# Forgetting heads: the mask moves from a matrix product to a GpSimd select, and the low parts of the probabilities move from VectorE to GpSimd

## The chip, the cores and the metric

The kernel runs on one core of one Trainium2 chip. The metric is the device time of one execution in microseconds (us). Three runs before the change took 1156.0, 1157.74 and 1158.17 us; their median is 1157.74. Engines are named as the profile names them: PE (TensorE, products), PEld (its weight loads), DVE (VectorE), ACT (ScalarE), POOL (GpSimd), SP (the queue that issues most DMAs).

## The reference

One decoder layer on 2048 tokens of width 1024: a normalised and modulated input goes through one input projection; eight forgetting-attention heads (FoX) and eight sliding-window heads run on it; their gated outputs go through one output projection and are added to the input. The change touches the forgetting heads only:

```python
cum = jnp.cumsum(jax.nn.log_sigmoid(f_logit), axis=1)      # per head
...
s = einsum('bhqd,bhkd->bhqk', qb, kh) * scale
s = s + cb[..., None] - cum[:, :, None, :]
causal = key_pos[None, :] <= q_pos[:, None]
s = jnp.where(causal, s, -jnp.inf)
p = jax.nn.softmax(s, axis=-1)
return einsum('bhqk,bhkd->bhqd', p, vh)
```

## The kernel before

The layer is computed in float32 accuracy with float16 operands: most values are split into a high part in float16 and a low part (the rest, also in float16), and a product is done as three (high by high, high by low, low by high). The program has a start (loads, norms), a stage of sliding-window heads, a stage of forgetting heads (some 462 to 1003 us) and the output projection.

The order of every engine's instructions is written out by hand. In the forgetting stage a loop (L1671) goes over 160 steps: 8 heads, in each 4 chunks of 512 queries, in each the pairs of 128-key blocks up to the diagonal (20 steps a head). A step's tile has keys on partitions and queries along the row. Its parts are methods of `Step`:

- `scores` (L1341): for each of the two key blocks two products into the score tile `sta` in PSUM, T with T (L1349) and the forget-gate rows (L1350). Where a block lies on the diagonal, a third product (L1352) of an identity `identb` and a constant `dmaskT`, both bfloat16, adds -1e30 to the masked scores of the 128x128 diagonal square. There is one score tile of two banks, so the next step's scores wait for this step's exponential.
- `exp32` (L1354): ACT turns the scores into float32 probabilities `p32` (called p in the profile; L1356). Three such tiles go round.
- `high` (L1358): ACT copies p to float16, the high part `pha` (L1360). Three tiles go round.
- `low` (L1362): DVE subtracts the high part from p and writes the low part beside it (L1363).
- `pv` (L1365): for each 128x128 block three products with the values (L1373, L1375 with the high part, L1376 with the low part).

Of the two blocks of a step either none lies on the diagonal (row width 1024) or both do; then the rows are cut to what the mask leaves, 512 + 384 = 896 or 256 + 128 = 384. Each chunk ends in one step of each of these two kinds, so 64 of the 160 steps are diagonal.

Step s runs in this order: exponential of s; low part of s-1; half of the filling work; high part of s; scores of s+1; products with values of s-2; the other half of the filling work. The filling work is projections of later heads (L351), row maxima (PE L1300, DVE L1303 and L1305), gates (ACT tanh L396, DVE L392, DMA of `z_d` from POOL L394), splits of weights (L273; ACT L1442 and DVE L1443 for the output weights) and, in head 7, the first output products (L1576). POOL's queue in this stage holds only DMA issues: weights (`wr`, L221), the maximum of a weight tile out to DRAM (`mx_d`, L230) and back to all partitions (`mxr`, L235), which waits for the first to land, pieces of a gate weight (`gw`, L1231), and `z_d`. In the sliding-window stage POOL also runs selects (L932, L934).

Of the kernel before, what the change touches and what calls it, by code (L numbers as in the profile page):

```python
# [10 lines left out]
F32 = mybir.dt.float32  # L11
F16 = mybir.dt.float16
BF16 = mybir.dt.bfloat16
I16 = mybir.dt.int16
I32 = mybir.dt.int32
AF = mybir.ActivationFunctionType
ALU = mybir.AluOpType
AX = mybir.AxisListType

P = 128  # L20
# [9 lines left out]
NEG = -1.0e30  # L30
# [5 lines left out]
XM, XR, VW = 66, 69, 129  # L36
# [7 lines left out]
def hybrid_layer(  # L44
# [17 lines left out]
    V, A, G, PE, SP = nc.vector, nc.scalar, nc.gpsimd, nc.tensor, nc.sync  # L62
# [12 lines left out]
    const = ctx.enter_context(tc.tile_pool(name="const", bufs=1))  # L75
# [78 lines left out]
    Shp = const.tile([P, KT], F32, name="Shp")  # L154

    ident = const.tile([P, P], F32, name="ident")
    identb = const.tile([P, P], BF16, name="identb")
    identh = const.tile([P, P], F16, name="identh")
    dmaskT = const.tile([P, P], BF16, name="dmaskT")
    lift = const.tile([P, 1], F32, name="lift")  # L160
    pfl = const.tile([P, 1], F32, name="pfl")
    csum = const.tile([P, 8, NB], F32, name="csum")
# [300 lines left out]
    start = ExitStack()  # L463
    st = start.enter_context(tc.tile_pool(name="start", bufs=1, reuse_waits="tile"))
    wad = start.enter_context(tc.tile_pool(name="wad", bufs=8, reuse_waits="tile"))
    with tc.manual_schedule():
# [23 lines left out]
            w_load(key, pieces(key))  # L490
        G.dma_start(snk[:], sinks[0].partition_broadcast(P))
        G.dma_start(bfg[:], b_fgate[0].partition_broadcast(P))
        V.tensor_copy(identb[:], ident[:])
        V.tensor_copy(identh[:], ident[:])
        PE.transpose(bk[0][:, :P], rows[:], ident[:])
        cols = st.tile([P, 40], F32, name="cols")
# [41 lines left out]
        zero = st.tile([P, P], F32, name="zero")  # L538
# [1 line left out]
        dm32 = st.tile([P, P], F32, name="dm32")  # L540

        G.affine_select(dm32[:], zero[:], [[-1, P]], ALU.is_ge, NEG, base=0, channel_multiplier=1)
        dm32t = st.tile([P, P], F32, name="dm32t")

        G.affine_select(dm32t[:], zero[:], [[1, P]], ALU.is_ge, NEG, base=0, channel_multiplier=-1)

        G.affine_select(triu[:], ones[:], [[1, P]], ALU.is_ge, 0.0, base=0, channel_multiplier=-1)

# [30 lines left out]
        A.activation(cs_[:], kh[:], AF.Sin)  # L579
        A.activation(sn_[:], sp_[:], AF.Copy, scale=-1.0)  # L580
        A.activation(dmask[:], dm32[:], AF.Copy)
        A.activation(dmaskT[:], dm32t[:], AF.Copy)

        def col8(name):
            return st.tile([P, KT], F32, name=name)
# [551 lines left out]
    with swa_order:  # L1137
# [10 lines left out]
        base = N_PRO  # L1148
# [182 lines left out]
    class Step:  # L1331
# [9 lines left out]
        def scores(self):  # L1341
            T, ci = Ts[self.hd % 2], self.ci
            self.st = ps_st.tile([P, 2 * CH], F32, tag="st", name="sta")
            for b, u0, o in self.blocks:
                w = CH - u0 * P
                kb_ = slice(b * P, (b + 1) * P)
                qc = slice(ci * CH + u0 * P, (ci + 1) * CH)
                diag = b >= 4 * ci
                PE.matmul(self.st[:, o:o + w], T[:, 3, kb_], T[:, 1, qc], start=True, stop=False)  # L1349
                PE.matmul(self.st[:, o:o + w], T[0:XR, 2, kb_], T[0:XR, 0, qc], start=False, stop=not diag)  # L1350
                if diag:
                    PE.matmul(self.st[:, o:o + P], identb[:], dmaskT[:], start=False, stop=True)  # L1352

        def exp32(self):  # L1354
            self.p32 = fxp.tile([P, 2 * CH], F32, tag="p32", name="p32")
            A.activation(self.p32[:, :self.w], self.st[:, :self.w], AF.Exp, scale=scl[f"qk{self.hd}"][:], bias=lift[:])  # L1356

        def high(self):  # L1358
            self.ph = fxh.tile([P, 2, 2 * CH], F16, tag="ph", name="pha")
            A.activation(self.ph[:, 0, :self.w], self.p32[:, :self.w], AF.Copy)  # L1360

        def low(self):  # L1362
            V.tensor_tensor(self.ph[:, 1, :self.w], self.p32[:, :self.w], self.ph[:, 0, :self.w], op=ALU.subtract)  # L1363

        def pv(self):  # L1365
            hd, ph = self.hd, self.ph
# [268 lines left out]
    with tc.manual_schedule():  # L1635
# [35 lines left out]
        for s, stp_ in enumerate(steps):  # L1671
# [11 lines left out]
            a = b = 0  # L1683
# [100 lines left out]
```

## Time and profile before

| what | value |
|---|---|
| median of three runs | 1157.74 us |
| profiled execution | 1157.8 us, of which its span 1156.1 us |
| share of the span | PE 97%, DVE 80%, ACT 57%, POOL 18% |
| granted clock of PE, mean | 0.996 |
| first and last exponential of the forgetting stage | 462.9 and 994.2 us |

The profile is one execution recorded instruction by instruction. A group row reads: line, engine, operation, output <- inputs, shapes, count | busy us, mean ns of one | idle time of the engine before them and what ended it. A row of a timeline reads: start, length, engine, line, operation, and in brackets how long the engine had been idle and who released it. A row of waits reads: who waited, for whom, us in total, times, longest. Products on PE are pipelined: the length of one is from its start to its end, and neighbours overlap.

### The profile page before, as it was taken

Reading aid. Unit: us, or ns where it says so; the run is one execution under the profiler, and the core shown is the slowest. Engines: PE = TensorE matmul, PEld = TensorE weight load, DVE = VectorE, ACT = ScalarE, POOL = GpSimd, SP = SyncE. Lnnn points to the kernel's source line nnn. Section 1 sums busy time; section 2 is a strip of 40 time slices with the busy share of each in tenths; the row PEclk is TensorE's granted clock in tenths of the full one; section 3 lists DMA queues with packets and bytes.
Section 4 is the critical chain, followed back from the end, with each engine's and each line's share of the span. In section 5 each row is a group of like instructions: output and inputs, shape, how many; then the busy total and the mean of one; then the engine's idle time right before and its main releaser. Section 6 shows DMA issues by size and latency. Waiting matters only on the chain. (4 is left out here: it accounts for less than half of the span.)

```text
span 1156.1 us, 25291 instructions
## 1 busy us (share of the span) xinstructions
PE 1116.8 (97%) x9869; PEld 656.3 (57%) x9869; DVE 930.5 (80%) x2137; ACT 661.4 (57%) x1150; POOL 207.5 (18%) x332
## 2 busy tenths in 40 slices
PE   5899999999999999999999999999999999999997
PEld 2475544577765866555555555555555555544444
DVE  7877468987888568788988899888888887878885
ACT  2876344654555421666757666666776778534332
POOL 1122134554556530010010110001000000000000
PEclk9899999999999999999999999999999999999999
DMA  9943355433243232442344342123311337686743
GB/s 333 336 116 72 87 78 96 97 63 90 52 92 88 58 87 58 73 108 29 80 64 87 84 67 70 38 49 76 45 43 34 91 101 206 140 225 197 199 135 109
DMA packets 123476, 120.10 MB, mean 104 GB/s; under 512 B 64948, under 2 KB 100828, under 8 KB 123356
## 3 DMA queue, kind: packets, MB, share of 16 engines
q1 hardware_dynamic: 112088, 85.69, 27.6%
q0 software_dynamic: 10832, 32.50, 13.5%
q8 instruction: 77, 1.26, 0.6%
q14 instruction: 43, 0.35, 0.1%
q10 hardware_dynamic: 436, 0.28, 0.1%
HBM read 64.75 MB, written 25.18 MB: 78 GB/s over the span
## 5 line engine op out<-in xcount | busy, mean ns | idle before, releaser
L1356 ACT ACTIVATE p<-sta,lift,scl_qk 128x1024 f32<-128x1024 f32 (+2 forms) x160 | 172.0, 1075 | 131.6 <-PE sta L1350 82.6
L351 PE MATMUL bk<-hT,wh_qk 128*128 128x512 f16 x768 | 194.7, 378 | 0.0
L1363 DVE TENSOR_TENSOR pha<-p,pha 128x1024 f16<-128x1024 f32 (+2 forms) x160 | 169.1, 1057 | 0.2 <-ACT pha L1360 0.2
L1303 DVE TENSOR_REDUCE a_m<-bk 128x1 f32<-128x512 f32 x192 | 130.4, 686 | 45.8 <-PE bk L1300 44.8
L1576 PE MATMUL bk<-wohl,oz 128*128 128x512 f16 x744 | 165.3, 379 | 1.1 <-DVE oz L1525 0.7
L1360 ACT ACTIVATE pha<-p 128x1024 f16<-128x1024 f32 (+2 forms) x160 | 148.1, 926 | 5.9 <-PE poa L1376 1.2
L1576 PEld LDWEIGHTS <-oz 128*128 128x128 f16 x744 | 71.9, 99 | 82.8 <-DVE oz L1525 1.8
L1376 PE MATMUL poa<-vt,pha 128*128 128x65 f16 x1088 | 116.1, 192 | 1.4 <-DVE pha L1363 1.2
L1373 PE MATMUL poa<-vt,pha 128*128 128x65 f16 x1088 | 116.6, 193 | 0.8 <-DVE ona L1382 0.7
L1375 PE MATMUL poa<-vt,pha 128*128 128x64 f16 x1088 | 116.6, 194 | 0.0
L351 PEld LDWEIGHTS <-wh_qk 128*128 128x128 f16 x768 | 72.1, 97 | 74.4 <-issue 2.1
L1349 PE MATMUL sta<-T 128*128 128x512 f16 (+1 forms) x320 | 110.9, 346 | 2.8 <-ACT p L1356 2.7
L1300 PE MATMUL bk<-T 66*128 66x512 f16 (+2 forms) x320 | 109.7, 348 | 2.4 <-DVE a_m L1303 1.9
L1373 PEld LDWEIGHTS <-pha 128*128 128x128 f16 x1088 | 101.5, 96 | 15.5 <-DVE ona L1382 1.9
L1350 PE MATMUL sta<-T 69*128 69x512 f16 (+1 forms) x320 | 109.8, 348 | 0.0
L1375 PEld LDWEIGHTS <-pha 128*128 128x128 f16 x1088 | 100.9, 97 | 11.4
L1376 PEld LDWEIGHTS <-pha 128*128 128x128 f16 x1088 | 100.8, 99 | 1.8 <-DVE pha L1363 1.7
L351 PE MATMUL bk<-hT,wh_za 128*128 128x512 f16 x384 | 99.7, 378 | 0.0
L369 PE MATMUL bk<-wh_va,hT 128*128 128x256 f16 x768 | 91.9, 273 | 0.0
L351 PE MATMUL bk<-hT,wh_zb 128*128 128x512 f16 x384 | 91.6, 379 | 0.2 <-DVE qc L754 0.2
L351 PE MATMUL bk<-hT,wh_qb 128*128 128x512 f16 x384 | 91.2, 379 | 0.0
L369 PEld LDWEIGHTS <-hT 128*128 128x128 f16 x768 | 73.3, 98 | 12.2 <-issue 2.1
(459 smaller groups left out, 1919.7 us busy)
## 6 DMA issues: line engine op xcount, KB each, us to landing
hT<-in_x_dram SPq DMA_DIRECT2D x20, 512.0 KB
wa<-in_w_ada_dram SPq DMA_DIRECT2D x16, 512.0 KB
z_d<-tz POOLq DMA_DIRECT2D x32, 256.0 KB, 3.0
T<-z_d SPq DMA_DIRECT2D x16, 512.0 KB
T<-stq SPq DMA_DIRECT2D x62, 128.0 KB
out_dram<-hT SPq DMA_DIRECT2D x15, 512.0 KB
xt<-in_x_dram SPq DMA_DIRECT2D x12, 512.0 KB
qs<-qf SPq DMA_DIRECT2D x80, 64.0 KB
```

Of the source, the lines that this page charges most:

```text
L351: PE.matmul(ps, whl[:, a, k, :], hT[ci][:, b, k, :], start=(k == 0 and n == 0), stop=(k == KT - 1 and n == 2))
L369: PE.matmul(ps[:, (u % 2) * 2 * P:(u % 2 + 1) * 2 * P], hT[ci][:, a, k, u * P:(u + 1) * P], wv[p][:, b, k, :], start=(k == 0 and n == 0), ...
L1303: V.tensor_reduce(m3[:, u, pc:pc + 1], mx[:, :w], axis=AX.X, op=ALU.max)
L1349: PE.matmul(self.st[:, o:o + w], T[:, 3, kb_], T[:, 1, qc], start=True, stop=False)
L1350: PE.matmul(self.st[:, o:o + w], T[0:XR, 2, kb_], T[0:XR, 0, qc], start=False, stop=not diag)
L1356: A.activation(self.p32[:, :self.w], self.st[:, :self.w], AF.Exp, scale=scl[f"qk{self.hd}"][:], bias=lift[:])
L1360: A.activation(self.ph[:, 0, :self.w], self.p32[:, :self.w], AF.Copy)
L1363: V.tensor_tensor(self.ph[:, 1, :self.w], self.p32[:, :self.w], self.ph[:, 0, :self.w], op=ALU.subtract)
L1373: PE.matmul(po[:, u, :], ph[:, 0, pq], vt[:, b, hd, 0:65], start=(self.first and n == 0 and u == 0), stop=False)
L1375: PE.matmul(po[:, u, 0:64], ph[:, 0, pq], vt[:, b, hd, 65:VW], start=False, stop=False)
L1376: PE.matmul(po[:, u, :], ph[:, 1, pq], vt[:, b, hd, 0:65], start=False, stop=(self.last and n == len(self.blocks) - 1))
L1576: PE.matmul(py, self.hl[:, i, k, :], w_slot(8 * j + k)[:, cc], start=(k == 0 and m_ == 0), stop=(k == KT - 1 and m_ == 2))
```

## The change

The mask product, its two constants and their preparation go. In a diagonal step POOL now sets the masked probabilities to zero in p, in float32, right behind the exponential: one `affine_select` over the two 128x128 squares. The low part is computed by POOL instead of DVE, at the same place in the program. The subtraction itself is the same.

```diff
-    identb = const.tile([P, P], BF16, name="identb")
-    dmaskT = const.tile([P, P], BF16, name="dmaskT")
...
-        V.tensor_copy(identb[:], ident[:])
...
-        dm32t = st.tile([P, P], F32, name="dm32t")
-        G.affine_select(dm32t[:], zero[:], [[1, P]], ALU.is_ge, NEG, base=0, channel_multiplier=-1)
...
-        A.activation(dmaskT[:], dm32t[:], AF.Copy)
...
-                diag = b >= 4 * ci
                 PE.matmul(self.st[:, o:o + w], T[:, 3, kb_], T[:, 1, qc], start=True, stop=False)
-                PE.matmul(self.st[:, o:o + w], T[0:XR, 2, kb_], T[0:XR, 0, qc], start=False, stop=not diag)
-                if diag:
-                    PE.matmul(self.st[:, o:o + P], identb[:], dmaskT[:], start=False, stop=True)
+                PE.matmul(self.st[:, o:o + w], T[0:XR, 2, kb_], T[0:XR, 0, qc], start=False, stop=True)
...
         def exp32(self):
             self.p32 = fxp.tile([P, 2 * CH], F32, tag="p32", name="p32")
             A.activation(self.p32[:, :self.w], self.st[:, :self.w], AF.Exp, scale=scl[f"qk{self.hd}"][:], bias=lift[:])
+            b, u0, o = self.blocks[1]
+            if b >= 4 * self.ci:
+                d = self.p32[:, 0:2 * o].rearrange("p (a c) -> p a c", a=2)[:, :, 0:P]
+                G.affine_select(d, d, [[0, 2], [1, P]], ALU.is_ge, 0.0, base=0, channel_multiplier=-1)
...
         def low(self):
-            V.tensor_tensor(self.ph[:, 1, :self.w], self.p32[:, :self.w], self.ph[:, 0, :self.w], op=ALU.subtract)
+            G.tensor_tensor(self.ph[:, 1, :self.w], self.p32[:, :self.w], self.ph[:, 0, :self.w], op=ALU.subtract)
```

The lines of the new kernel are a few lower: scores L1341 and L1342, exponential L1346, select L1350, high part L1354, low part L1357, products with values L1367, L1369 and L1370.

PE, the scores of the first step, a diagonal one (sta is the score tile, T the queries, keys and gate rows of a head). Before:

```order
L1349 MATMUL sta<-T_6055 128x512
L1350 LDWEIGHTS T_6055
L1350 MATMUL sta<-T_6055 128x512
L1352 LDWEIGHTS identb
L1352 MATMUL sta<-dmaskT,identb 128x128
L1349 LDWEIGHTS T_6055
L1349 MATMUL sta<-T_6055 128x384
```

And after:

```order
L1341 MATMUL sta<-T_6047 128x512
L1342 LDWEIGHTS T_6047
L1342 MATMUL sta<-T_6047 128x512
L1341 LDWEIGHTS T_6047
L1341 MATMUL sta<-T_6047 128x384
```

The mask product and its weight load are gone from between the two blocks; nothing else moved.

POOL, the first steps of head 0, before: the write of a weight maximum, gate weight, read-back, gate output and so on (names as above).

```order
L230 DMA mx_d_76<-w_mx 128x1
L1231 DMA gw_6569<-in_w_ada_dram 128x1024
L235 DMA mxr<-mx_d_76 128x128
L394 DMA z_d<-tz 128x512
L1231 DMA gw_6936<-in_w_ada_dram 128x1024
```

And after, the same place, where p is the float32 probabilities and pha the high and low parts:

```order
L228 DMA mx_d_76<-w_mx 128x1
L1224 DMA gw_6558<-in_w_ada_dram 128x1024
L1350 AFFINE_SELECT p_6560<-p_6560 128x2x128
L1357 TENSOR_TENSOR pha<-p_6518,pha 128x896
L1357 TENSOR_TENSOR pha<-p_6560,pha 128x384
L1357 TENSOR_TENSOR pha<-p_6583,pha 128x1024
L233 DMA mxr<-mx_d_76 128x128
L1350 AFFINE_SELECT p_6682<-p_6682 128x2x128
L1357 TENSOR_TENSOR pha<-p_6632,pha 128x1024
L1350 AFFINE_SELECT p_6729<-p_6729 128x2x128
```

Between the write of a weight maximum and its read-back there now stand a select and three low parts, and the select of a step stands ahead of the low part of the step before (p_6682 ahead of p_6632).

ACT, the last two diagonal steps of head 6, with what each instruction waits for. Before:

```order
L1356 ACTIVATE p_13452<-sta,lift,scl_qk_11210 128x896 [waits DVE_49,PE_49]
L1442 ACTIVATE wohl<-sv,wsc 128x512 [waits DMAHW4_49]
L1360 ACTIVATE pha<-p_13452 128x896 [waits PE_49,Activation_49]
L1261 ACTIVATE rw<-bk_136 8x128 [waits DVE_49,PE_49]
L1356 ACTIVATE p_13496<-sta,lift,scl_qk_11210 128x384 [waits DVE_49,PE_49]
```

And after:

```order
L1346 ACTIVATE p_13388<-sta,lift,scl_qk_11164 128x896 [waits PE_49,Pool_49]
L1436 ACTIVATE wohl<-sv,wsc 128x512 [waits DMAHW4_49]
L1354 ACTIVATE pha<-p_13388 128x896 [waits PE_49,Pool_49]
L1254 ACTIVATE rw<-bk_134 8x128 [waits DVE_49,PE_49]
L1346 ACTIVATE p_13431<-sta,lift,scl_qk_11164 128x384 [waits PE_49]
```

ACT's order is the same; the exponential gets its p tile back from POOL instead of DVE, and the high part waits for POOL's select.

## The prediction

> **What bounds the kernel now.** I read the first page, then the busy time by stretches, then the rows of PE, ACT, DVE and POOL around the changed lines. The page's head and one query of two stretches come first; the columns of the second are the stretch, its length, and busy us (with counts) of PE, PEld, DVE, ACT and POOL, then clock and DMA.
>
> ```profile
> span 1156.1 us, 25291 instructions
> PE 1116.8 (97%) x9869; PEld 656.3 (57%) x9869; DVE 930.5 (80%) x2137; ACT 661.4 (57%) x1150; POOL 207.5 (18%) x332
> ```
>
> ```profile
> core 0: us, PE busy (x) PEld busy (x) DVE busy (x) ACT busy (x) POOL busy (x), PEclk, DMA share, GB/s
> 462.00:1003.00 541.00, 532.96 (x5517) 310.75 (x5516) 467.62 (x1018) 380.17 (x465) 35.55 (x57) 1.00 0.35 76
> 916.00:932.00 16.00, 12.99 (x190) 8.38 (x188) 15.86 (x30) 15.06 (x21) 0.00 (x0) 1.00 0.38 101
> ```
>
> All edited work lies in the forgetting heads, 462 to 1003 us. There PE is busy 532.96 of 541 us: PE sets the pace, DVE has 73 us of idle time, ACT 161, POOL 505. The second row is an exception: in the 16 us at the end of head 6, with little projection work left to fill PE, DVE (15.86) and ACT (15.06) are full and PE is not (12.99). The granted clock is 1.00 in both, so it enters no term.
>
> **What goes from PE.** The mask products are one group of 128 (8 heads, 16 diagonal blocks). Its 219 ns is the length of one from start to end; what one costs PE is the distance between starts. The second fence is PE's timeline (start, length, instruction) in one diagonal step.
>
> ```profile
> L1352 PE MATMUL sta<-dmaskT,identb x128: 219/219/220, 462.2 to 993.9; 128*128 128x128 bf16 x128
> ```
>
> ```profile
> 475.31 0.22 PE L1352 MATMUL sta<-dmaskT,identb 128*128 128x128 bf16 x1
> 475.37 0.32 PE L1349 MATMUL sta<-T 128*128 128x384 f16 x1
> 475.53 0.33 PE L1350 MATMUL sta<-T 69*128 69x384 f16 x1
> 475.69 0.22 PE L1352 MATMUL sta<-dmaskT,identb 128*128 128x128 bf16 x1
> 475.75 0.19 PE L1373 MATMUL poa<-vt,pha 128*128 128x65 f16 x1
> ```
>
> ```profile
> 1013.90 10.38 PE bk L1576 x48
> ```
>
> From 475.31 to 475.37 and from 475.69 to 475.75: 0.06 us by rows rounded to 0.01; as a 512-column product takes 0.216 (10.38 / 48, the third fence, from the chain of waits), a 128-column one should take 0.054. I take 0.057: 128 x 0.057 = **7.3 us**, all on the bounding engine except where PE already waits. In the stretch 916 to 932 the products at the heads' border (8 of them, 0.5 us) free nothing, since ACT and DVE are last there. That leaves 6.8.
>
> **What goes from DVE.** The low parts:
>
> ```profile
> L1363 DVE TENSOR_TENSOR pha<-p,pha 128x1024 f16<-128x1024 f32 (+2 forms) x160 | 169.1, 1057 | 0.2 <-ACT pha L1360 0.2
> PE bk L1300 <- DVE a_m L1303: 1.9, 5, 0.7
> PE poa L1376 <- DVE pha L1363: 1.2, 2, 0.6
> PE poa L1373 <- DVE ona L1382: 0.7, 1, 0.7
> PE bk L1257 <- DVE lk L1277: 0.5, 1, 0.5
> ```
>
> DVE loses 169.1 of its 467.62 us, but PE waits for DVE only 1.9 + 1.2 + 0.7 + 0.5 = 4.3 us in this stage. So the big removal is worth between 0 and 4.3 us; I book 0 and keep 4.3 for the low end.
>
> **What comes to POOL.** The nearest rows are POOL's own selects of the sliding-window heads (64 each, one input), and a small float32 one; the widths of the 160 exponentials are the widths of the low parts.
>
> ```profile
> L934 POOL TENSOR_SCALAR_AFFINE_SELECT ptb<-fold 128x512 f16<-128x512 f16 x64 | 48.3, 754 | 0.0
> L932 POOL TENSOR_SCALAR_AFFINE_SELECT ptb<-fold 128x512 f16<-128x512 f16 x64 | 45.6, 713 | 20.2 <-ACT fold L927 15.4 <-DVE fold L928 4.7
> L542 POOL TENSOR_SCALAR_AFFINE_SELECT dm<-zero 128x128 f32<-128x128 f32 x1 | 0.3, 287 | 0.9 <-DVE zero L539 0.9
> ```
>
> ```profile
> L1356 ACT ACTIVATE p<-sta,lift,scl_qk x160: 648/1204/1209, 462.9 to 994.2; 128x1024 f32<-128x1024 f32 x96, 128x896 f32<-128x896 f32 x32, 128x384 f32<-128x384 f32 x32
> ```
>
> The widths make 96 + 32 x 0.875 + 32 x 0.375 = 136 full widths of 1024. The new select covers 256 float32 elements: between 0.287 (128 elements) and 0.73 (512), by a straight line 0.44; 64 of them, 28 us. A subtraction of 1024 with two inputs is not in the trace. From below: two selects of 512, 1.45 us, as if the second input were free; from above: twice that, 2.9 us, as if each input cost a pass. I take 2.2, the middle, because one row bounds both ends and nothing favours either. Then POOL carries 136 x 2.2 + 28 + its present 35.55 = 363 of 541 us (260 to 458 at the ends). It stays a side engine in the mean; what counts is whether each low part is in time. One step's rows, on ACT, DVE and PE in turn:
>
> ```profile
> 642.02 1.04 ACT L1360 ACTIVATE pha<-p 128x1024 f16<-128x1024 f32 x1
> ```
>
> ```profile
> 646.64 1.22 DVE L1363 TENSOR_TENSOR pha<-p,pha 128x1024 f16<-128x1024 f32 x1
> ```
>
> ```profile
> 651.29 0.19 PE L1376 MATMUL poa<-vt,pha 128*128 128x65 f16 x1
> ```
>
> The high part ends at 643.06, but DVE, behind with its maxima, reaches the low part 3.6 us later and ends at 647.86; PE uses it at 651.29. POOL, idle, could start at 643.1 and end at 645.3 (646.0 at the upper price), before DVE does now. So the slower engine delivers earlier, and the low parts cost PE **0**. That cover, 6 us from 645.3 to 651.29, is also what hides the DMA issues among which the low parts now stand; the worst of them is the read-back of a weight maximum, which holds POOL's queue until its write lands:
>
> ```profile
> POOL mxr L235 <- DMA mx_d<-w_mx: 84.6, 20, 9.0
> ```
>
> The mean is 84.6 / 20 = 4.2 us, inside the 6; the longest, 9.0, is counted from a POOL that came early, and now two or three low parts of 2.2 us stand between write and read. I book 0, at worst 3 us once or twice. The last two steps have nothing behind them: the final select and two low parts queue up on POOL, and the last but one ends some 0.4 us after PE wants it. **+0.4.**
>
> The Trainium skill speaks against the move: its page "GPSIMD Engine Reference", section "Performance versus the Vector engine", keeps elementwise work off this engine and gives 4497 ns for a float32 tensor_tensor of 2048, against 2293 on the other engine. An estimate from that page is 2.25 us per 1024, with which POOL's load would be 370 us and the forecast the same; no row of this case shows it yet.
>
> **The added wait.** In the 64 diagonal steps the high part on ACT now waits for the select on POOL: 0.44 us and two hand-overs, some 0.6, more if a low part is still running. Behind it on ACT stand the next exponential, the copies and the tanh of the gates; PE waits for the exponential through the one score buffer. ACT mostly waits for PE itself:
>
> ```profile
> ACT p L1356 <- PE sta L1350: 82.6, 74, 2.8
> ACT p L1356 <- PE sta L1352: 44.3, 41, 4.6
> ```
>
> This idle time, 127 us, swallows 64 x 0.6 = 38 us where both fall in the same step. Where ACT has none, they show. The rows of ACT, then one of PE, at the end of head 6:
>
> ```profile
> 926.13 1.10 ACT L1356 ACTIVATE p<-sta,lift,scl_qk 128x896 f32<-128x896 f32 x1
> 927.11 0.72 ACT L1442 ACTIVATE wohl<-sv,wsc 128x512 f16<-128x512 f32 x1
> 927.72 0.95 ACT L1360 ACTIVATE pha<-p 128x896 f16<-128x896 f32 x1
> 928.57 0.25 ACT L1261 ACTIVATE rw<-bk 8x128 f16<-8x128 f32 x1
> 928.72 0.65 ACT L1356 ACTIVATE p<-sta,lift,scl_qk 128x384 f32<-128x384 f32 x1
> ```
>
> ```profile
> 927.28 0.27 PE L1349 MATMUL sta<-T 128*128 128x256 f16 x1 [0.65 <-ACT p L1356]
> ```
>
> ACT runs without a gap, though a weight split of 0.72 lies between exponential and high part and hides about that much. I charge 0.6 for each of the two diagonal steps there and 0.6 for one more near the end: **+1.8**.
>
> The three instructions that go from the start (a select, a cast and a copy of 128 columns, some 0.3 us each by the 0.287 row) lie among loads that PE waits for; 0, at most 0.3 gained.
>
> **Sum.** The profiled execution took 1157.8, its span 1156.1 and 1.7 around it; the median of the three runs is 1157.74, so nothing has to be shifted. 1157.8 - 6.8 + 0.4 + 1.8 = 1153.2, so **1153**. With the 4.3 us of DVE waits regained as well it is 1149.
>
> **Rivals.**
> 1. *POOL becomes the pace (slower).* Place: its queue of 160 low parts. The point from which it decides: (541 - 28 - 35.55) / 136 = 3.5 us per full width. At 3.7 POOL needs 136 x 3.7 + 64 = 567, so 26 us more than the stage: 1184. Against it: both ends, 1.45 and 2.9, lie under 3.5; for it: no two-input row of any width exists. 0.14.
> 2. *ACT's waits come through.* If a third of the 38 us reaches PE, 12.7 - 6.8 makes 1164; from 6.8 us on the gain is gone. For it: ACT is 70% busy in the stage and in order; against it: the 127 us of waiting for PE. 0.14, of which 0.04 ends within the bound.
> 3. *DVE and POOL hold each other up* where both read two operands from SBUF. Two such DVE rows, a gate sum and a weight split:
>
> ```profile
> 649.52 1.28 DVE L1237 SCALAR_TENSOR_TENSOR gacc<-gw,sil,gacc 128x1024 f32<-128x1024 f32 x1
> ```
>
> ```profile
> 927.96 0.74 DVE L1443 SCALAR_TENSOR_TENSOR wohl<-sv,wsc,wohl 128x512 f16<-128x512 f32 x1
> ```
>
> They would wait for up to a whole low part, 2.2. Say twice with PE behind them and the border of head 6 kept as full as now: +4.4, 1158. For it: DVE instructions with two SBUF operands in most steps; against it: DVE has just lost 169 us. 0.08. This is the lock that the Trainium skill describes on its page "SBUF — State Buffer", section "Who interferes with whom": a VectorE instruction with two SBUF inputs and a GpSimd one that reads SBUF exclude each other for a whole instruction. No row of this case shows such a pair.
> 4. *The 128 products were not on the path.* Then 1157. Against it: PE's 532.96 of 541, and starts that follow at 0.06. 0.06.
>
> **Chances.** The forecast, 1149 to 1155, has 0.58. A measurement of this kernel tells about 0.2%, 2.3 us, from no change. Faster: 0.58. Same: 0.04 + 0.08 + 0.06 = 0.18. Slower: 0.14 + 0.10 = 0.24. The range takes in the forecast, rivals 3 and 4 and rival 2 up to its 1164, and leaves out rival 1: 1149 to 1164.
>
> **What would show it.** Right: no dmaskT products, PE's instruction count down by 128, its busy time in the stage down about 7 and still above 97% of it; low parts on POOL near 2.2 us, starting within 0.1 of the high part's end; no PE wait on POOL over 1 us in total before the last two steps; high parts waiting for POOL some 0.6 us in the diagonal steps, and ACT's wait for scores down by as much. Wrong: low parts over 3.5 us and PE waiting for them at L1370 of the new kernel (rival 1); PE waiting for exponentials by more than 5 us (rival 2); DVE's two-operand groups longer than now (rival 3).

## The result, and the profile after

The changed kernel took 1171.8 us (median of 4 runs, 1170.48 to 1172.31) against 1157.74 before: a ratio of 1.0122, 95% interval 1.0106 to 1.0138. That is 14.1 us slower; I had forecast 1153 in a range up to 1164. The page of the new kernel begins so:

```profile
span 1169.8 us, 25195 instructions
PE 1117.4 (96%) x9741; PEld 652.5 (56%) x9741; DVE 890.4 (76%) x1976; ACT 660.5 (56%) x1149; POOL 529.0 (45%) x555
```

The 128 products are gone (9869 to 9741), and DVE lost 161 instructions, 160 of them low parts. But DVE's busy time fell by only 40 us (930.5 to 890.4), although the low parts alone had taken 169.1. That is the first line to stop at.

Next the stretch from the first to the last exponential, by the busy time of the engines. First before, then after; below the whole stretch of after stand the four places at which its clock fell (columns: stretch, length, then busy us with counts of PE, PEld, DVE, ACT and POOL, granted clock, DMA share, GB/s).

```profile
462.86:994.19 531.33, 523.90 (x5408) 304.85 (x5407) 460.54 (x996) 377.78 (x461) 35.55 (x57) 1.00 0.34 75
```

```profile
461.57:1008.65 547.08, 524.98 (x5295) 301.27 (x5294) 420.52 (x842) 377.21 (x460) 352.32 (x278) 0.99 0.31 72
492.00:496.00 4.00, 1.58 (x4) 0.56 (x4) 3.71 (x9) 1.95 (x2) 1.55 (x1) 0.77 0.43 131
496.00:500.00 4.00, 4.00 (x37) 2.27 (x36) 1.43 (x3) 2.67 (x4) 1.38 (x2) 0.80 0.41 82
664.00:668.00 4.00, 3.43 (x9) 1.26 (x9) 3.68 (x11) 0.00 (x0) 2.77 (x2) 0.60 0.96 228
668.00:672.00 4.00, 4.00 (x43) 2.40 (x42) 1.70 (x4) 1.83 (x2) 1.17 (x2) 0.97 0.62 169
744.00:748.00 4.00, 1.90 (x27) 1.04 (x24) 3.83 (x9) 1.72 (x3) 1.28 (x2) 0.84 0.23 53
748.00:752.00 4.00, 4.00 (x36) 2.61 (x35) 2.92 (x6) 1.38 (x3) 1.30 (x3) 0.73 0.23 53
972.00:976.00 4.00, 2.01 (x12) 1.06 (x13) 3.79 (x4) 2.05 (x3) 0.84 (x1) 0.93 0.59 210
976.00:980.00 4.00, 4.00 (x35) 2.62 (x33) 1.05 (x4) 3.54 (x6) 2.50 (x2) 0.64 1.00 334
```

The stretch grew by 15.75 us. PE's idle time in it grew from 7.4 to 22.1 us (length less busy). Its busy time did not fall but rose by 1.1, though 128 products are gone: at four places PE ran at a lower clock. Each pair of rows loses the same: (1 - 0.77) x 4 + (1 - 0.80) x 4 = 1.72 us, and 1.72 again for each of the other three, 6.9 in all. Before, every stretch of 4 us in this stage stands at 1.00.

What did DVE do with the time it was given? Five groups of DVE in the stage, before and after: the low limb of the output, the two scalings of the row maxima, a maximum of two 128x1 columns, and the maxima themselves, which read PSUM (count | busy us, mean ns).

```profile
L291 DVE TENSOR_TENSOR oh<-ona,oh 128x256 f16<-128x256 f32 x24 | 10.0, 418 | 0.0
L1317 DVE TENSOR_SCALAR lq<-a_m 128x4 f16<-128x4 f32 x29 | 4.9, 170 | 1.0
L1320 DVE TENSOR_SCALAR lq<-a_mr 128x4 f16<-128x4 f32 x29 | 4.9, 170 | 1.0
L250 DVE TENSOR_TENSOR w_pw<-w_pw,pfl 128x1 f32<-128x1 f32 x6 | 1.0, 159 | 0.2
L1303 DVE TENSOR_REDUCE a_m<-bk 128x1 f32<-128x512 f32 x175 | 118.9, 686 | 43.1 <-PE bk L1300 42.1 <-ACT p L1356 0.4
```

```profile
L289 DVE TENSOR_TENSOR oh<-ona,oh 128x256 f16<-128x256 f32 x24 | 30.5, 1270 | 0.2 <-ACT oh L293 0.2
L1310 DVE TENSOR_SCALAR lq<-a_m 128x4 f16<-128x4 f32 x29 | 28.1, 970 | 1.0
L1313 DVE TENSOR_SCALAR lq<-a_mr 128x4 f16<-128x4 f32 x29 | 19.0, 654 | 1.0
L248 DVE TENSOR_TENSOR w_pw<-w_pw,pfl 128x1 f32<-128x1 f32 x6 | 13.6, 2274 | 0.2
L1296 DVE TENSOR_REDUCE a_m<-bk 128x1 f32<-128x512 f32 x174 | 117.3, 685 | 61.3 <-PE bk L1293 58.3 <-ACT p L1346 2.8 <-issue 0.2
```

An instruction on four columns went from 170 to 970 ns, one on a single column from 159 to 2274, with the same operands and sizes; the maxima stayed at 685. All groups together, low parts left out, DVE's instructions in the stage are 114 us longer; below this is called DVE's excess. What grew reads and writes SBUF alone (most with two operands there, the scalings with one); what reads PSUM did not grow, nor did one-operand instructions on a single column (154 ns before and after). One such instruction on DVE, what POOL did meanwhile, and what PE did next (start, length, instruction, idle time before it and releaser):

```profile
488.85 4.73 DVE L248 TENSOR_TENSOR w_pw<-w_pw,pfl 128x1 f32<-128x1 f32 x1
...
494.22 0.14 DVE L1298 DVE_READ_ACCUMULATOR2_ANT a_m<- 128x1 f32 x1
```

```profile
486.68 4.22 POOL L1357 TENSOR_TENSOR pha<-p,pha 128x1024 f16<-128x1024 f32 x2
490.85 0.55 POOL L1224 DMA_DIRECT2D gw<-in_w_ada_dram  x1
491.42 2.13 POOL L1357 TENSOR_TENSOR pha<-p,pha 128x1024 f16<-128x1024 f32 x1
```

```profile
494.42 1.44 PE L349 MATMUL bk<-hT,wh_za 128*128 128x512 f16 x3 [2.47 <-DVE a_m L1298]
495.65 0.63 PE L1341 MATMUL sta<-T 128*128 128x512 f16 x1
```

DVE's one-column maximum starts while POOL is in the second of two subtractions, stays open through the DMA issue and a third subtraction, and ends at 493.58, within 0.03 us of that subtraction's end (493.55). The maxima queued behind it on DVE come late, the banks they would free come late, and PE stands for 2.47 us. Then its clock falls: products of 512 columns take 0.63 instead of 0.38. PE's larger waits in the stage of after (who, for whom: us in total, times, longest):

```profile
PE bk L1250 <- DVE lk L1270: 5.0, 5, 2.3
PE sta L1341 <- ACT p L1346: 4.9, 8, 1.0
PE bk L1293 <- DVE a_m L1296: 4.1, 3, 2.6
PE bk L1570 <- DVE oz L1519: 2.8, 1, 2.8
PE bk L349 <- DVE a_m L1298: 2.5, 1, 2.5
```

With four smaller rows they make 21.8 us, 16.7 of them for DVE (4.8 before). None is for POOL: the low parts themselves are always in time.

### The profile page after: what moved, and what is told of

It is laid out like the page before. It is cut to its first block, busy times and chain, and to the rows that moved or that the text cites. A ratio compares the mean times of both kernels' runs of the same rounds, so it can differ in the third digit from the quotient of the medians.

```text
span 1169.8 us, 25195 instructions
## 1 busy us (share of the span) xinstructions
PE 1117.4 (96%) x9741; PEld 652.5 (56%) x9741; DVE 890.4 (76%) x1976; ACT 660.5 (56%) x1149; POOL 529.0 (45%) x555
## 4 chain that ended last, share of the span: by engine, by line
PE 69%; DVE 15%; ACT 5%; issue 4%; DMA 4%; POOL 2%; SPq 0%; ACTq 0%; DVEq 0%; POOLq 0%
PE bk L349 26%; PE bk L1570 12%; PE bk L367 7%; PE bk L1293 4%; PE sta L1341 4%; PE sta L1342 4%; PE poa L1369 2%; PE poa L1367 2%; PE poa L1370 2%; DMA wa<-in_w_ada_dram 2%; PE pss L882 1%; PE pob L939 1%; DVE a_m L1296 1%; ACT p L1346 1%; PE pxb L911 1%
## 5 line engine op out<-in xcount | busy, mean ns | idle before, releaser
L1357 POOL TENSOR_TENSOR pha<-p,pha 128x1024 f16<-128x1024 f32 (+2 forms) x160 | 295.8, 1860 | 32.4 <-ACT pha L1354 30.4
L1346 ACT ACTIVATE p<-sta,lift,scl_qk 128x1024 f32<-128x1024 f32 (+2 forms) x160 | 171.8, 1074 | 105.9 <-PE sta L1342 103.0
L1354 ACT ACTIVATE pha<-p 128x1024 f16<-128x1024 f32 (+2 forms) x160 | 148.2, 926 | 43.9 <-POOL p L1350 41.0
L1367 PE MATMUL poa<-vt,pha 128*128 128x65 f16 x1088 | 117.6, 194 | 0.0
L1369 PE MATMUL poa<-vt,pha 128*128 128x64 f16 x1088 | 117.3, 195 | 0.0
L1370 PE MATMUL poa<-vt,pha 128*128 128x65 f16 x1088 | 117.1, 193 | 0.0
L1341 PE MATMUL sta<-T 128*128 128x512 f16 (+1 forms) x320 | 110.2, 349 | 5.0 <-ACT p L1346 4.9
L1367 PEld LDWEIGHTS <-pha 128*128 128x128 f16 x1088 | 102.3, 97 | 13.9 <-issue 0.2
L1369 PEld LDWEIGHTS <-pha 128*128 128x128 f16 x1088 | 101.8, 98 | 14.0 <-issue 0.3
L1342 PE MATMUL sta<-T 69*128 69x512 f16 (+1 forms) x320 | 108.9, 351 | 0.0
L1370 PEld LDWEIGHTS <-pha 128*128 128x128 f16 x1088 | 101.5, 99 | 0.1
```

What stands on the lines that cost most here:

```text
L1357: G.tensor_tensor(self.ph[:, 1, :self.w], self.p32[:, :self.w], self.ph[:, 0, :self.w], op=ALU.subtract)
L1367: PE.matmul(po[:, u, :], ph[:, 0, pq], vt[:, b, hd, 0:65], start=(self.first and n == 0 and u == 0), stop=False)
L1369: PE.matmul(po[:, u, 0:64], ph[:, 0, pq], vt[:, b, hd, 65:VW], start=False, stop=False)
L1370: PE.matmul(po[:, u, :], ph[:, 1, pq], vt[:, b, hd, 0:65], start=False, stop=(self.last and n == len(self.blocks) - 1))
```

## The experiments

Three theories went in. A: DVE and POOL exclude each other in SBUF, and DVE's held instructions reach PE. B: ACT's wait for the select reaches PE. C: the low parts come late out of POOL's queue. Every ratio is against runs of the kernel before on the same chip; microseconds are the ratio times 1157.74.

| kernel | ratio, 95% interval | change, us |
|---|---|---|
| the change | 1.0122, 1.0106 to 1.0138 | +14.1 |
| e1: mask part alone | 0.9996, 0.9986 to 1.0007 | -0.5 |
| e2: low parts alone | 1.0159, 1.0138 to 1.0180 | +18.4 |
| e3: low parts in halves | 1.0069, 1.0048 to 1.0089 | +8.0 |
| e4: DVE's held instructions altered or moved | 1.0301, 1.0280 to 1.0322 | +34.8 |
| e5: no products, no select | 0.9955, 0.9943 to 0.9968 | -5.2 |
| e6: select behind the low part | 0.9977, 0.9968 to 0.9986 | -2.7 |
| e7: diagonal low parts alone | 1.0039, 1.0027 to 1.0052 | +4.5 |
| e8: high part in pieces | 1.0005, 0.9994 to 1.0015 | +0.6 |
| e9: two DMAs to SP's queue | 1.0063, 1.0049 to 1.0076 | +7.3 |
| e11: one DMA later | 1.0065, 1.0053 to 1.0078 | +7.5 |
| e12: the same, in the stage only | 0.9985, 0.9976 to 0.9994 | -1.7 |
| e13: an extra copy on POOL | 1.0078, 1.0063 to 1.0093 | +9.0 |

### The two halves of the change, apart

e1 is the changed kernel with the low parts back on DVE; e2 the kernel before with only the low parts on POOL.

```diff
 # e1, against after
-            G.tensor_tensor(self.ph[:, 1, :self.w], self.p32[:, :self.w], self.ph[:, 0, :self.w], op=ALU.subtract)
+            V.tensor_tensor(self.ph[:, 1, :self.w], self.p32[:, :self.w], self.ph[:, 0, :self.w], op=ALU.subtract)
 # e2, against before: the same line the other way round
```

> Select on POOL kept, low parts back on DVE. Theory A (DVE and POOL shut each other out while POOL subtracts two operands, 114 us of extra DVE time in the changed kernel's trace): with only 64 selects of 0.41 us on POOL the extra DVE time falls under 10 us, PE's idle time in the stage is back near 8 us, and the 7 us of mask products show: about 1151. Theory B (ACT's wait for the select, 41 us in the trace of the changed kernel, is what reaches PE): this wait stays, so the time stays at 1165 or above. Theory C (low parts come too late from POOL's queue): 1151 too; the next run tells it from A.

> Low parts on POOL, masks as products on PE as before. Theory A: the loss of the changed kernel with no mask saving, 1171.8 + 7 = 1179, with the extra DVE time again over 100 us, in instructions that end at the moment a subtraction on POOL ends, and no wait of PE for a low part. Theory B: no select, so no loss: about 1158. Theory C: about 1179 too, but PE's waits for low parts would be over 10 us.

e2 took 1177.37 us and e1 1158.21. So the whole loss comes with the low parts, and with them DVE's excess: 104 us in e2, 3.4 in e1 (there and in the other kernels that keep low parts on DVE, what these grew is counted in). In e2 PE again never waits for POOL, which takes C out. That e1 came out level instead of at 1151 was the second open question; e5, e6, e8, e9, e11 and e12 go after it.

e2 also separates the loss from the clock. In its profiled execution (1173.93, the shortest of four) the granted clock is 1.00 over the whole stage, and still PE's idle time there is 22.7 us, 17.4 of it waits for DVE. So the waits alone make the kernel some 15 us slower; what the clock takes comes on top. The mean granted clock of e2's four executions goes from 0.994 in the shortest to 0.988 and 0.987 in the two longest.

### Is it the lock? Dose, halves, one operand, other instructions

e7 leaves the mask on PE and moves only the diagonal steps' low parts.

```diff
 # e7, against before
-            V.tensor_tensor(self.ph[:, 1, :self.w], ...)
+            E = G if self.blocks[1][0] >= 4 * self.ci else V
+            E.tensor_tensor(self.ph[:, 1, :self.w], ...)
```

> The kernel before (mask products on TensorE) with only the diagonal steps' low parts on GpSimd: 64 of the 160 subtractions, 29% of their columns. If GpSimd's subtraction holds VectorE whenever it runs, the loss goes with its time: 29% of the 18.7 us that all 160 cost gives about 1163, and VectorE's other instructions grow by about 30 us instead of 104. If only long or back-to-back subtractions do harm, 1158 and an excess under 15 us.

It lost 4.5 us, and DVE's excess was 31 us, 6 of it on the low parts that stay on DVE. Both go roughly with POOL's share of the subtractions: 29% of 18.4 is 5.3, of 104 is 30.

e3 splits each low part on POOL into two instructions, so that DVE could get in between.

```diff
 # e3, against after
-            G.tensor_tensor(self.ph[:, 1, :self.w], self.p32[:, :self.w], self.ph[:, 0, :self.w], op=ALU.subtract)
+            for c0 in range(0, self.w, self.w // 2):
+                cc = slice(c0, c0 + self.w // 2)
+                G.tensor_tensor(self.ph[:, 1, cc], self.p32[:, cc], self.ph[:, 0, cc], op=ALU.subtract)
```

> Changed kernel with each low part as two subtractions of half the width on POOL, about 1.1 us each. If the hold ends with every POOL instruction and DVE then gets its turn (theory A, plain), the mean wait of a DVE instruction halves, the extra DVE time falls from 114 to about 60 us and the time to about 1160. If POOL takes its next instruction before DVE gets in (theory A, with DVE starved across neighbours, as one DVE instruction spanned two subtractions in the trace of the changed kernel), the extra DVE time stays near 114 and the time at 1172 or above. Theory B: no change, 1172.

Its time lies between the two that I had named: it is 6 us faster than the change (PE's waits for DVE are 11.6 us instead of 16.7), but most of the excess stays, 99 us of 114. Three of the groups shown above, in e3:

```profile
L289 DVE TENSOR_TENSOR oh<-ona,oh 128x256 f16<-128x256 f32 x23 | 29.0, 1260 | 0.2 <-ACT oh L293 0.2
L1310 DVE TENSOR_SCALAR lq<-a_m 128x4 f16<-128x4 f32 x29 | 18.2, 628 | 1.0
L248 DVE TENSOR_TENSOR w_pw<-w_pw,pfl 128x1 f32<-128x1 f32 x6 | 15.6, 2594 | 0.2
```

The two-operand ones are held as long as with whole subtractions (1270 and 2274 ns there). A DVE instruction held by one POOL instruction does not get in before the next that stands ready behind it; only the scalings profit from the shorter piece.

e13 keeps the whole kernel before and adds work on POOL that nobody needs: the same probabilities copied to float16, one operand instead of two.

```diff
 # e13, against before (scr: a float16 tile of 512 columns)
             V.tensor_tensor(self.ph[:, 1, :self.w], ...)
+            for c0 in range(0, self.w, self.w // 2):
+                G.tensor_copy(scr[:, :self.w // 2], self.p32[:, c0:c0 + self.w // 2])
```

> The kernel before, all of it, and beside each low part (still on VectorE) GpSimd copies the same float32 probabilities to float16 into a scratch tile that nobody reads, in two halves: an instruction with one source where the change's subtraction has two. No engine waits for it except for the release of the p tile. If any GpSimd work in SBUF holds VectorE, the excess of VectorE's two-operand instructions is that of the low parts moved (104 us) or more, since VectorE's 160 subtractions stay, and the time is 1175 to 1200. If only GpSimd's two-source instructions hold it, VectorE's durations stay and the time is 1157.7.

Neither end held. It lost 9.0 us, and the excess is 33 us: 15.5 on the low parts that stay on DVE, 17.5 on the other groups. Two of these:

```profile
L1365 DVE TENSOR_TENSOR pha<-p,pha 128x1024 f16<-128x1024 f32 x96 | 129.4, 1347 | 0.2 <-ACT pha L1362 0.2
L291 DVE TENSOR_TENSOR oh<-ona,oh 128x256 f16<-128x256 f32 x23 | 15.7, 683 | 0.0
```

Copies hold DVE too, but on the same groups less: 17.5 us for 228 us of copies, against 114 for 296 us of subtractions in the change, or 0.08 us against 0.39 for each us of POOL. The number of operands is not the only difference, though: DVE's own low parts still run here, take 15.5 us of the holds themselves and hold the copies in turn (of 512 columns, 0.61 us undisturbed and up to 1.66). The time of this kernel is not the lock alone: its stage also began 3.2 us later (466.04) and its DMA issues on POOL stood behind the copies. How the 9.0 us divide stays open.

e4 attacks the held instructions instead: the scalings of the row maxima, the low limb of the output and the gate sums go to POOL, two one-column instructions take their second operand as a per-partition scalar.

```diff
 # e4, against after
-            V.tensor_tensor(pw[:], pw[:], pfl[:], op=ALU.max)
+            V.tensor_scalar(pw[:], pw[:], pfl[:], None, op0=ALU.max)
...
-            V.tensor_scalar(lq_[:, 0:4], m4, -1.0 / XA, None, op0=ALU.mult)
+            G.tensor_scalar(lq_[:, 0:4], m4, -1.0 / XA, None, op0=ALU.mult)
...
-            V.tensor_tensor(oh[:, :, 1], on, oh[:, :, 0], op=ALU.subtract)
+            G.tensor_tensor(oh[:, :, 1], on, oh[:, :, 0], op=ALU.subtract)
```

> Changed kernel with the DVE instructions that were held longest given another form: rescaling of the row maxima (29 times, three small ones each), low parts of the head outputs (24) and the gate sums (8) go to POOL; two products of single columns take one operand as a scalar. POOL still carries all low parts. Theory A: the extra DVE time falls from 114 to under 25 us (weight splits and the key rows are left), PE idles about 8 us in the stage, and the time is 1150 to 1154, below both kernels. Theory B and theory C: still 1168 or above, C even more, since POOL has some 40 us more to do.

My largest miss among the runs: 1193.44. The excess did fall, to 36 us, and the one-column maximum with a scalar operand took 214 ns where it had taken 2274. But now POOL is late, the theory C that the change itself had cleared. In e4:

```profile
ACT pha L1357 <- POOL p L1353: 80.7, 54, 7.2
PE sta L1344 <- ACT p L1349: 18.0, 18, 5.0
PE poa L1373 <- POOL pha L1360: 11.8, 6, 3.1
```

A select stands behind a gate sum's two instructions (2.85 and 2.83 us) in POOL's queue, ACT waits for it up to 7.2 us, and PE for ACT. Here, moving the held instructions to the engine that holds them traded one queue for the other. So no run shows what the change would take without the hold and with POOL on time.

### Where the products' 7 us went

e5 takes the products out of the kernel before and puts nothing in their place; it leaves the causal mask out.

```diff
 # e5, against e1
-            b, u0, o = self.blocks[1]
-            if b >= 4 * self.ci:
-                d = self.p32[:, 0:2 * o].rearrange("p (a c) -> p a c", a=2)[:, :, 0:P]
-                G.affine_select(d, d, [[0, 2], [1, P]], ALU.is_ge, 0.0, base=0, channel_multiplier=-1)
...
-        V.tensor_copy(cmask[:, 3 * P:], dmask[:])
+        V.memset(cmask[:, 3 * P:], 0.0)
```

> The kernel before with the 128 mask products taken out and nothing in their place: no select, low parts on VectorE. It leaves out the causal mask inside the diagonal blocks (the row maxima take the masked squares too, so that all stays finite). It prices the products alone. If they stand on the path as I forecast, 1157.7 - 6.8 = about 1151 us, PE's busy time in the stage about 526 us and its waits as before (8 us). If they are hidden (my fourth rival), 1157 to 1158, with PE's waits longer by the 7 us.

It gained 5.2 us (3.7 to 6.6). The products stand on the path; PE's busy time between the first and the last exponential fell from 523.90 to 517.62, its idle time rose by 1.4. So in e1 4.7 us of that are lost again, and something that the select brings must have eaten them. e6 takes the select out of ACT's way: after the low part, on both float16 halves.

```diff
 # e6, against e5
             V.tensor_tensor(self.ph[:, 1, :self.w], ...)
+            b, u0, o = self.blocks[1]
+            if b >= 4 * self.ci:
+                for l in range(2):
+                    d = self.ph[:, l, 0:2 * o].rearrange("p (a c) -> p a c", a=2)[:, :, 0:P]
+                    G.affine_select(d, d, [[0, 2], [1, P]], ALU.is_ge, 1.0, base=0, channel_multiplier=-1)
```

> The kernel above with GpSimd's selects put back, but later: two per diagonal step, on the float16 high and low parts, behind the subtraction on VectorE, so that ScalarE never waits for a select and only the product p v does. It leaves out the causal mask (the fill is 1 and the row maxima take the masked squares). If the first kernel of this series (mask change alone, 1158) lost its 7 us because ScalarE's high part waits for the select, this one comes out near the kernel without selects, about 1151 to 1153. If GpSimd's selects cost the time by being there (holding VectorE), it stays near 1157 to 1159, and VectorE's instructions in the stage are longer by some 10 us or more.

-2.7 us, between e5 and e1, with DVE's excess at 1.5 us: the selects hold nobody much. PE's waits for exponentials, first in e1, then in e6 (e5 has the same row), and the wait that e6 has in their place:

```profile
PE sta L1341 <- ACT p L1346: 7.3, 12, 1.0
```

```profile
PE sta L1341 <- ACT p L1346: 2.9, 6, 0.7
PE poa L1368 <- POOL pha L1358: 2.2, 2, 1.2
```

So the wait behind ACT takes a part of the gain (B): with it out of the way about half of the 4.7 us comes back. Is it that a select and its two hand-overs are long? e8 tests that, with the masked squares' high part last, so that the select runs beside the rest.

```diff
 # e8, against e1, in the diagonal steps
-            A.activation(self.ph[:, 0, :self.w], self.p32[:, :self.w], AF.Copy)
+            for c0, c1 in ((P, o), (o + P, self.w)):
+                if c0 < c1:
+                    A.activation(self.ph[:, 0, c0:c1], self.p32[:, c0:c1], AF.Copy)
+            A.activation(hd_, pd, AF.Copy)
```

> The mask change alone (selects on GpSimd, low parts on VectorE), and on the diagonal steps the high part in two or three activations: the columns outside the masked squares first, the squares last, so that the select runs beside the first ones. This adds 96 activations of 128 to 384 columns to ScalarE. If ScalarE's wait for the select is what ate the 7 us, the wait (44 us) falls to some 15 and the time to 1152 to 1155. If the gain is lost elsewhere it stays at 1158, or rises where the added activations reach PE.

It stayed level. ACT's waits for the select fell from 44 to 18 us, as expected, but PE's wait for exponentials only from 7.3 to 6.3. Of the 26 us that ACT no longer waits, 12 go into 96 more activations, and the waits that PE feels are others. They stand in rows of e1. POOL, then ACT, then PE at the start of head 3:

```profile
670.09 0.58 POOL L228 DMA_DIRECT2D mx_d<-w_mx  x1 [3.64 <-DVE w_mx L225]
670.68 1.10 POOL L1350 TENSOR_SCALAR_AFFINE_SELECT p<-p 128x256 f32<-128x256 f32 x1
```

```profile
668.00 0.67 ACT L1346 ACTIVATE p<-sta,lift,scl_qk 128x384 f32<-128x384 f32 x1 [0.58 <-PE sta L1342]
671.82 0.52 ACT L1354 ACTIVATE pha<-p 128x384 f16<-128x384 f32 x1 [3.14 <-POOL p L1350]
672.25 1.19 ACT L1346 ACTIVATE p<-sta,lift,scl_qk 128x1024 f32<-128x1024 f32 x1
```

```profile
673.48 0.38 PE L1341 MATMUL sta<-T 128*128 128x512 f16 x1 [0.31 <-ACT p L1346]
```

The exponential ended at 668.67. The select could have run then, but POOL stood at the issue of a weight maximum's write (mx_d) until DVE had that maximum, and began the select at 670.68, 2.0 us late; it then took 1.10 instead of 0.41, while a low part ran on DVE. ACT waited 3.14 us, the next exponential came late, and PE stood. Five selects of e1 were 2.0 to 2.7 us late in this way, four behind mx_d (once with a gate weight's issue between) and one behind the write of a gate's output (z_d), and five of PE's waits follow them.

e11 issues mx_d two ticks later, behind the select; e9 gives mx_d and z_d to SP; e12 is e11 inside the attention stage only.

```diff
 # e11, against e1 (e12: only once the stage has begun)
-        G.dma_start(md[:], mx[:])
+        after(2, lambda: G.dma_start(md[:], mx[:]))
 # e9, against e1
-        G.dma_start(md[:], mx[:])
+        SP.dma_start(md[:], mx[:])
-                G.dma_start(z_d[kt, :, ci * CH:(ci + 1) * CH], t[:])
+                SP.dma_start(z_d[kt, :, ci * CH:(ci + 1) * CH], t[:])
```

> The mask change alone (1158.2), with one edit: GpSimd issues the write of a weight maximum (mx_d) two ticks, about one step, later, so that in each head's first diagonal steps the select stands ahead of it in GpSimd's queue. In the trace of the mask change alone five selects started 2.0 to 2.7 us late behind such a DMA issue that waited for VectorE (at 531.88, 603.80, 670.68, 740.54 and, behind a z_d write, 949.02), and five of PE's six waits for ScalarE's exponentials beyond those without selects follow them within 3 us (0.89, 0.85, 0.31, 0.96, 0.94). If that queue is what ate the mask's gain, the first four waits go: 3.0 us, and the clock dip of 1.7 us may go or stay: 1154 to 1155.5. If the plain length of the chain exponential, select, high part does it, nothing changes: 1158.

> The mask change alone (1158.2), with both kinds of DMA that held the selects (the maxima's writes mx_d and the gates' writes z_d) issued by SyncE instead of GpSimd. If GpSimd's queue ate the gain, all five late selects and their PE waits (4.0 us) go: 1153.5 to 1155, near the kernel with late selects (1155.0). If SyncE's queue, which waits for these DMAs' data in turn, holds up the transfers of the next head's q and k (T<-stq, T<-rw), PE gets new waits for T or a_m and the time stays at 1158 or rises above it.

> As the later mx_d write (1165.7), but with the write moved only inside the attention stage; in the stages before it stays where it was. In the later-write kernel the time from the first to the last exponential fell from 533.8 us (mask change alone) to 530.3, as I expected, but that stage began 10.5 us later, because the same edit held up the weights of the stages ahead of it. With those left alone the stage should begin near 462.5 again and the time come out 3.5 us under the mask change alone: 1154 to 1155.5, which is under the kernel before (1157.7). If the time stays at 1158, the selects' queue is not what ate the mask's gain.

e11 and e9 both lost 7 us, and before this stage: their first exponential came at 472.84 and 470.78 instead of 462.26. In e11 that is because the same line serves the weights of all stages before: within the stage it took 530.32 us from first to last exponential, 3.5 less than e1's 533.82, and e12 confirms it, with the start at 462.54, the stage at 530.41 and the time at 1156.07. For e9 the cause of the late start is not tested. The same place in e12, POOL and then ACT, and its wait row:

```profile
667.45 0.41 POOL L1354 TENSOR_SCALAR_AFFINE_SELECT p<-p 128x256 f32<-128x256 f32 x1 [2.29 <-ACT p L1350]
668.80 0.58 POOL L230 DMA_DIRECT2D mx_d<-w_mx  x1 [0.94 <-DVE w_mx L226]
```

```profile
667.89 0.52 ACT L1358 ACTIVATE pha<-p 128x384 f16<-128x384 f32 x1 [0.51 <-POOL p L1354]
```

```profile
PE sta L1345 <- ACT p L1350: 4.3, 8, 0.9
```

The select starts at once and ACT waits 0.51. Leaving aside e5 and e6, which leave the mask out, e12 is the one kernel clear of before on the fast side: by 1.7 us (0.7 to 2.8). Against e1, measured beside other runs of before, the intervals of the two ratios overlap; that the DMA's place matters is shown by the stage in two kernels (3.4 and 3.5 us shorter) rather than by the medians.

The queue is not all that e1 lost. In its profiled execution the clock also fell once, at the end of head 6:

```profile
926.00:930.00 4.00, 2.73 (x32) 1.55 (x32) 4.00 (x8) 3.49 (x7) 1.41 (x2) 0.89 0.05 16
930.00:934.00 4.00, 4.00 (x48) 2.87 (x47) 4.00 (x6) 2.02 (x3) 1.17 (x1) 0.68 0.23 68
```

By the same sum as above that is 1.72 us again. e12 has such a fall at the same place (0.58 in 926 to 930), and e9 has one there too; the profiled executions of e5, e6, e8 and e11 have none in the stage. In e1 and e12 no wait of PE near it is over 0.7 us. Why the clock falls there in some of these kernels is open.

## Why the prediction was wrong, point by point

By the runs the change divides into three steps, one after the other: products out, -5.2 us (e5); selects in, +4.7 (e1 less e5); low parts to POOL, +14.6 (the change less e1). The split depends on the order: with the low parts moved first they cost +18.4 (e2), and the mask's part is then worth -4.3 (the change less e2) instead of e1's -0.5.

- **The products, -6.8.** Right, a little large: -5.2, with 6.8 just outside the interval (3.7 to 6.6). My fourth rival is out.
- **DVE's removal, 0.** Not shown either way: no run takes the low parts off DVE without putting them on POOL, and there PE's waits for DVE grow for another reason.
- **POOL's prices.** Right: I took 2.2 us for a low part and 28 us for the selects; the traces have 2.13 undisturbed and 27.8, and POOL's load in the stage was 357 us (I said 363). POOL is not the pace; rival 1 is out. The Trainium skill's figure, from "GPSIMD Engine Reference", section "Performance versus the Vector engine", from which I had estimated 2.25, also agrees. That no two-input row of any width existed was wrong (L116, 128x4, 0.20 us), but so short a row would not have priced 1024 columns.
- **"So the slower engine delivers earlier, and the low parts cost PE 0."** This step failed: instead of 0 the low parts cost +14.6, and +18.4 when they alone are moved. Its premise held: no wait for a low part. What it left out is what POOL's subtraction does to DVE while it runs. That was my third rival, whose sign (longer two-operand groups on DVE) is what the rows show, and its price failed too: "up to a whole low part, 2.2", twice, +4.4. Measured, a DVE instruction of 0.16 us took up to 6.21, since several POOL instructions in a row may hold it, and the scalings with one operand are held too. PE waited for DVE by over 1 us seven times (never before). Over the stage DVE's excess is 114 us; PE's waits for DVE rose from 4.8 to 16.7, and the clock took 6.9 more. I counted against this rival that DVE had lost 169 us of work. That spare time does not help: the held instruction blocks DVE's queue at a moment when the maxima behind it are due.
- **"No row of this case shows such a pair."** Wrong, and the trace of the kernel before could have corrected the price. In its sliding-window stage POOL's selects run beside DVE instructions with two SBUF operands. L765 has 20 of them with a median of 0.69 us; one took 2.92, while four selects ran back to back (the DVE row, then the first and the last select):

```profile
190.96 2.92 DVE L765 TENSOR_TENSOR qc<-qc,qs 128x512 f32<-128x512 f32 x1
```

```profile
190.92 0.65 POOL L932 TENSOR_SCALAR_AFFINE_SELECT ptb<-fold 128x512 f16<-128x512 f16 x1
192.69 0.63 POOL L934 TENSOR_SCALAR_AFFINE_SELECT ptb<-fold 128x512 f16<-128x512 f16 x1
```

Both surprises of the change are in these rows: the hold goes on over several POOL instructions, and one operand on POOL's side is enough.
- **The clock, which "enters no term".** Wrong for the profiled execution of the change: four waits of 2.1 to 2.8 us were each followed by a fall that cost PE 1.72 us, beside the wait itself. It need not happen: e2's three waits of 2.5 to 2.8 us had no fall behind them.
- **The added wait, +1.8.** In the changed kernel the mechanism and the size were right: ACT waits 41.0 us for selects (I had said 38), and PE's waits for exponentials rose from 2.7 to 4.9, so by 2.2. The place was right in part: +0.7 at the end of head 6, +0.5 later, +1.0 at the start of a head. In e1, with the low parts on DVE, it was mis-sized: +4.7 in all, of which 4.6 us of PE's waits (2.7 to 7.3), and most of them at the starts of heads, where a DMA that waits for DVE stands ahead of the select in POOL's queue; at the end of head 6 PE's waits are those of before, and the clock fell instead. The prediction followed POOL's queue for the low parts and not for the selects. Part of my second rival, then, with a cause I had not named. The change itself has only two selects over 2 us late, against e1's five, which fits the order of the steps above; why it has fewer I have not followed.
- **The tail, +0.4.** Not seen: from the last exponential to the end it was 161.9 us before and 161.2 after.

Of the 15.75 us by which the stage grew, PE's busy time gives +1.1 (products -6.3 by e5, clock +6.9, 0.5 left over) and its idle time +14.7, all of it in waits named above (21.8 less 7.1 in the same stretch). The half microsecond I have not followed.

On the mechanism, the Trainium skill, "SBUF — State Buffer", section "Who interferes with whom", says that a VectorE instruction with two SBUF inputs excludes a GpSimd one that reads SBUF, that some one-input forms do so when they use both ports, and that the one that waits is blocked for the whole instruction of the other. The trace agrees (ends within 0.03 us, PSUM readers untouched at 685 ns), and shows more: the block may go on into the next POOL instruction. Which port is held no run here shows.

## What to carry to other kernels

Before moving elementwise work from DVE to POOL, search the whole trace, other stages too, for places where the two engines already run side by side, and compare the longest DVE instruction of a group there with the median. Then list what stays on DVE with its operands in SBUF, and look at what is queued behind each such instruction: the price is not the slower engine's time but DVE's queue held for one or more whole POOL instructions, and it grew with POOL's share of the subtractions (29% gave 4.5 of 18.4 us). Before putting a short instruction on POOL into another engine's chain, read which DMA issues stand ahead of it in POOL's queue and what those wait for. And when a line that issues a DMA is moved, look at every stage that uses the line: the edit that gained 3.5 us in one stage lost 10 in an earlier one.

## What the runs showed of the hardware that was not expected

- A DVE instruction held by POOL stays held over several POOL instructions: 4.73 us over a subtraction, a DMA issue and another subtraction, for an instruction of 0.16. Halving POOL's instructions did not shorten it (2274 and 2594 ns on average).
- The hold goes both ways, but unevenly: a select on POOL took 1.10 us instead of 0.41 while a subtraction ran on DVE.
- POOL instructions with one operand hold DVE too: a DVE addition of 0.69 us took 2.92 over four selects. On average the copies of e13 held DVE's other groups about a fifth as much as the subtractions did, for the same POOL time (0.08 against 0.39), beside low parts that stayed on DVE.
- After four waits of PE of 2.1 to 2.8 us the clock fell, and each fall cost 1.72 us by the rows above, as 3.44 us at half clock would. The Trainium skill, "TensorE: Matmul & The Clock Gate", section "What's actually happening", gives half clock and free-running windows of about 3.4 us; the loss agrees with one such window. It names an idle window of that length as the cause; here the waits were shorter than it, a wait of 2.31 us at 604.34 and e2's of 2.47, 2.56 and 2.77 had no fall behind them, and in e1 the clock fell with PE busy 2.73 of 4 us and no wait over 0.7.
